# Decoder trunk on one core: pooled loads issued by the ACT queue three products apart, the last pooling mixer and the embedding inputs some products later

## The chip, the cores and the metric

The kernel runs on one core of a Trainium2 chip. The metric is the device time of one execution in microseconds (us). TensorE is called PE, VectorE DVE, ScalarE ACT, GpSimd POOL and SyncE SP. SP computes nothing here: it issues DMA transfers. ACT and POOL also issue some transfers, in the order in which their own instructions stand. PE multiplies weights that it loads 128x128 at a time with moving tiles of 128x512 elements.

## The reference, cut to what matters

A sequence of 1024 tokens of width 2048 goes through one layer. Names are those of the kernel, where `u` is the pooling mixer's input, `gp` and `ga` are the gates of the pooling and of the attention branch, and `cc` is the concatenated input of the output projection.

```python
h = x @ w_in + b_in
q, k, v, g_attn, u_pool, g_pool = split(h)
a = banded_sink_attention(q, k, v, sinks, bias, valid) * silu(g_attn)
b = multiscale_pool(u_pool, w_pool, pool_scale) * silu(g_pool)
mix = concatenate([a, b]) @ w_out
ple = sigmoid(x @ w_gate_ple) * (p @ w_ple)
out = layer_norm(ALPHA * x + mix + ple, ln_gain, ln_bias)
```

`multiscale_pool` subtracts each channel from its trailing mean over 2, 4, 8 or 16 tokens (four groups of 256 channels), maps each group with a 256x256 matrix of its own and scales the channels. All of it is in float32.

## The kernel before, in words

**Products.** A float32 product is made of three: each operand is split into a high part, which ACT casts (`wh`, `b11h`, `t1h`, ...), and a low part, which DVE gets by a subtraction (`wl`, `b11l`, ...). `mm3` (L179 to L181) issues high by high, low by high and high by low. Above this lies one level of Strassen's scheme in Winograd's form: two blocks of 128 output columns (a *job*) take seven products instead of eight. The right-hand operand is kept as seven sets with the names `b11`, `b21`, `t1`, `t2`, `t3`, `b22`, `t4`, and the left-hand (weight) operand is made for each job by DVE additions on the loaded `raw` tiles, followed by the split into `wh` and `wl` (`make_unit`). One product is a run of 12 matmuls of 128x512 into one PSUM bank (`qa` or `qb`). It is gathered into an SBUF tile `part`: the first one by an ACT copy (L346), the others by DVE additions (L122).

**Order.** A group is one job alone or two jobs side by side. `run_group` issues the products of a group one after the other, and after each of them a clock ticks. All other work is tied to that clock: `after(n, f)` calls `f` n products later, and `later(n, f)` does the same and also keeps what `f` issues behind the latest gathering instructions. A scheduler then puts the instructions of each engine in a row, so that a number of products says where a piece of work may stand, and the engine's queue, in order, says what stands behind it.

**The stage around the change.** Half 0 of the sequence goes through the last input projections (`gp`, `u`), then through eight `wgate` groups (the sigmoid gate of the embedding), then through `ga0` and `ga1` alone and `ga2`, `ga3` side by side. After that half 1 of `w_out` is multiplied by a right-hand set built from `cc4` to `cc7`, the *pooled set*.

* `pool_u` (L612) makes the trailing means of one group of channels. On its second call of a group it sets four things by the clock: a load of the map `wpool` and its split, a load of the gates (`s<-sgp`), and `mix(g)` (L641). `mix` is 24 matmuls (`sc<-e`), four DVE products (L653), and four stores that POOL issues (`cc<-s`). The last of the mixers is that of g = 1. The gates come from `gate_pool` (L604): ACT takes the silu of the finished `gp` tile, and SP stores it (`sgp<-part`).
* `embed_in` (L659) loads the four tiles of `p` (`s<-in_p`), two products apart, and splits them (L669 and DVE). `rest` multiplies them by `w_ple` (`sc<-e`) one to four products after a `wgate` group has ended; `embed_ahead` loads `x` for it (`s<-in_x`).
* The pooled set is built by `set_from` (L255): `begin` sets four fetches of two 512 KB tiles each (`two<-cc`, L267) by the clock, and the steps `s0` to `s4` split them (`b11h`, ...) and subtract them (`two<-two,two`). `pooled()` is called ahead of the last group but two, so that the loads fall into the groups `ga1` and `ga2`/`ga3`.
* `gate_ahead` loads the attention's results (`s<-pre`), and `gate_attn` (L597) takes silu and multiplies (DVE `part<-s,part`), after the DMA-accumulated first half has come in (`part<-h`, L359, issued by POOL).

**Slots.** The `s` tiles are 16 slots used in turn, and in the stage of the pooled set six smaller ones; `e` tiles are six. A load into a slot waits for the last reader of what lay there, and where that was a transfer, for its end. `raw` tiles and `wh`/`wl` tiles are used in turn as well.

Of the kernel before, what the change touches and what calls it, by code (L numbers as in the profile page):

```python
# [32 lines left out]
T = 512  # L33
# [30 lines left out]
class Layer:  # L64
# [78 lines left out]
    def fetch(self, src, extra=False):  # L143
        s = self.extra() if extra else self.slot()
        return self.load(s[:, : src.shape[-1]], src)

    def split(self, src, extra=False):
        n = src.shape[-1]
        hi, lo = ((self.extra if extra else self.slot)(F32R)[:, :n] for _ in range(2))
        self.nc.scalar.copy(out=hi, in_=src)  # L150
        self.lo(lo, src, hi)
        return hi, lo
# [10 lines left out]
    def later(self, n, fn):  # L163

        def run():
            with ExitStack() as ctx:
                for ins in self.latest.values():
                    ctx.enter_context(self.tc.issue_after(ins))
                fn()
        self.after(n, run)  # L170
# [81 lines left out]
    def two(self):  # L252
        return self.tile(self.twos, [P, 2, self.F], "two")

    def set_from(self, get, F, keep=None, first=None, by=None):  # L255

        nc = self.nc
        r = {}

        def fetch(u, part=None):  # L260
            h, k = int(u[2]) - 1, 2 * (int(u[1]) - 1)
            if not part:
                r[u] = [self.two() for _ in range(2)]
            for i, t in enumerate(r[u]):
                src = get(h, k + i)
                if part is None:
                    (by or (nc.sync if first else nc.scalar)).dma_start(out=t, in_=src)  # L267
                elif i == 0 and part < 2:
                    self.load(t[:, part], src[:, part])
                elif i == 1 and part == 2:  # L270
                    self.load(t, src)

        def sub(u, a, b, place):
            out = []
            for k in range(2):
                o = r[place][k] if place else self.two()
                self.tt(o, r[a][k], r[b][k], ALU.subtract)
                if keep:
                    self.load(keep[u][k], o)
                out.append(o)  # L280
            r[u] = out

        split = lambda u: self.split_unit(u, r[u])

        def begin():
            self.F = F
            if first:
                first(fetch)
                return
            for i, u in enumerate(("b11", "b21", "b12", "b22")):  # L290
                self.later(1 + 2 * i, lambda u=u: fetch(u))

        def s0():
            if first:
                a, b = r["b11"]
                self.split_unit("b11", [a[:, 0], a[:, 1], b])
            else:
                split("b11")

        def s1():  # L300
            split("b21")
            sub("t1", "b12", "b11", "b11")

        def s2():
            split("t1")
            sub("t2", "b22", "t1", None if keep else "t1")

        def s3():
            split("t2")
            sub("t3", "b22", "b12", "b12")  # L310

        def s4():
            split("t3")
            sub("t4", "b21", "t2", "b21")

        return [begin, s0, s1, s2, s3, s4, lambda: split("b22"), lambda: split("t4")]

    def set_kept(self, get, keep):
# [289 lines left out]
    def pool_u(self, j, c):  # L608
        nc, g = self.nc, j // 2
        w = 2 << g  # L610
        out = []
        for h in range(2):  # L612
            u = self.slot()
            if h == 0:
                nc.gpsimd.memset(u[:, 0:16], 0.0)
            else:
                self.ident_act(u[:, 0:16], c[:, 0, T - 16 :], self.c(C_BIN + U0 + j))
            self.ident_act(u[:, 16:], c[:, h], self.c(C_BIN + U0 + j))
            cur, d, first = u, 1, 1
            while d < w:  # L620
                nxt = self.slot()
                end = 2 * d == w
                f = 16 if end else first
                self.tt(nxt[:, f:], cur[:, f:], cur[:, f - d : T + 16 - d], ALU.add)
                cur, d = nxt, 2 * d
                first = first + d
            if h == 0:
                self.tt(cur[:, 16 : 16 + 16], cur[:, 16 : 16 + 16], self.c(C_HEAD + 16 * g, 16), ALU.mult, nc.gpsimd)
            nc.vector.scalar_tensor_tensor(out=cur[:, 16:], in0=cur[:, 16:], scalar=1.0 / w, in1=u[:, 16:],
                                           op0=ALU.mult, op1=ALU.subtract)  # L630
            out.append(self.split(cur[:, 16:], 2 * (j % 2) + h < 3))
        self.diff[j] = out
        if j % 2:
            f = slice((g % 2) * T, (g % 2) * T + T)
            self.after(4, lambda: self.got.update({("wp", g): self.fetch(self.wpool[g // 2][:, f])}))
            self.later(8, lambda: self.got.update({("wp", g): self.split(self.got["wp", g])}))
            late = 3 if g == 1 else 0
            self.after(6 + late, lambda: self.got.update({("sg", g): [[self.fetch(self.sgp[2 * g + e][:, h * T : h * T + T]) for e in range(2)] for h in range(2)]}))
            self.later(10 + late // 2, lambda: self.mix(g))

    def mix(self, g):  # L641
        nc = self.nc
# [182 lines left out]
    def run(self):  # L825
        nc, tc, fix = self.nc, self.tc, self.fix
# [28 lines left out]
        ga, gp, u = ([(win, *p) for p in pairs(b, 4)] for b in (GA0, GP0, U0))  # L855
# [60 lines left out]
        for o in reversed(BESIDE):  # L916
            u = UNITS[o]
# [61 lines left out]
        g = 2  # L979
# [13 lines left out]
        t = 9  # L993
# [12 lines left out]
        g += n2  # L1006


        pooled, *make_pooled = self.set_from(lambda h, k: self.cc[4 + k][:, :, h * T : h * T + T], T, by=nc.sync)
        for i in range(n3):  # L1010
            if i == 1:
                over.close()
                over = ExitStack()
                self.extras = self.work_pool("e2", 6, over)
            if self.groups[g + i + 1][0][0].b[0] == 0 and i < n3 - 2:
                self.after(5, self.embed_in)
                self.after(7, lambda: self.embed_w(0))
            if i == n3 - 2:

                over.close()  # L1020
                work.close()
                work = ExitStack()
                self.slot_n = T
                self.slots = self.work_pool("slots1", 6, work)
                self.twos = self.work_pool("twos1", 8, work)
                pooled()
                for n, step in enumerate(make_pooled):
                    self.after(10 + 3 * n, step)
                for n, b in enumerate(b for j in s3[-2:] for b in j.b):
                    self.after(14 + 2 * n, lambda b=b: self.gate_ahead(b - GA0))  # L1030
            self.run_group(g + i, () if i else steps)
# [86 lines left out]
        for k in range(4):  # L1118
            r = rest_x[k]
            f = slice((k % 2) * 2 * F2, (k % 2) * 2 * F2 + 2 * F2)  # L1120
            h, l = (t[k // 2][:, f].rearrange("p (k t) -> p k t", k=2) for t in (hi, lo))
# [92 lines left out]
```

## Time and profile before

| | |
|---|---|
| time before, median of 3 | 1492.81 us (1492.71 to 1498.43) |
| profiled execution, its own time | 1498.43 us |
| its span, first to last instruction | 1496.7 us |
| PE busy | 1450.5 us, 97% of the span |
| DVE, ACT, POOL busy | 75%, 52%, 19% |
| mean granted TensorE clock | 0.990 of full speed |

The profiled execution is the slowest of the three, 5.62 us above the median. Busy is the time in which an engine had an instruction. A matmul of 128x512 is listed with 0.39 us, while the next starts some 0.227 us later, since they are pipelined: start times are what is to be compared. In brackets behind a row stands how long the engine was idle before it, and what released it. A row with x2 stands for two such instructions one after the other.

### The profile page before, as it was taken

The numbers are of one execution on the slowest core, as the hardware profiler recorded it, in microseconds if no ns is written. First come the engines' busy times: TensorE is split into PE (matmuls) and PEld (weight loads), VectorE is DVE, ScalarE is ACT, GpSimd is POOL, SyncE is SP. The second block draws the span as 40 slices with busy tenths as digits, with TensorE's granted clock in tenths as the row PEclk, the third lists the DMA queues.
The fourth block names the chain that finished last, engine by engine and source line by source line (L and its number), as shares of the span: only waits on it lengthen the run. The fifth ranks groups of instructions, "written<-read, shape, count | busy, mean of one in ns | idle before, by whom it ended". The sixth has DMA issues, their size and how long they took to land. (4 is left out here: it accounts for less than half of the span.)

```text
span 1496.7 us, 20472 instructions
## 1 busy us (share of the span) xinstructions
PE 1450.5 (97%) x6972; PEld 1224.6 (82%) x6972; DVE 1120.8 (75%) x2030; ACT 780.7 (52%) x1550; POOL 277.7 (19%) x388
## 2 busy tenths in 40 slices
PE   8999999999999999999999999999999999999986
PEld 6788888888887888888887778888877888899985
DVE  7788578888787877888677956565579566987785
ACT  5354656655666555666634443333356333555484
POOL 0000123322333332231111110000011111111240
PEclk9999999999999999999999999999999999999998
DMA  7563975445445554557856666575696667585463
GB/s 262 190 218 102 258 197 191 148 150 184 171 171 176 170 188 174 174 191 250 197 140 202 158 219 190 170 193 166 197 295 183 172 187 224 146 231 137 155 230 137
DMA packets 101721, 280.38 MB, mean 187 GB/s; under 512 B 11632, under 2 KB 16880, under 8 KB 101616
## 3 DMA queue, kind: packets, MB, share of 16 engines
q1 hardware_dynamic: 78576, 204.09, 40.1%
q0 software_dynamic: 19712, 67.64, 19.5%
q10 hardware_dynamic: 3328, 7.34, 1.5%
q8 instruction: 55, 0.90, 0.2%
q14 instruction: 50, 0.41, 0.1%
HBM read 193.04 MB, written 85.98 MB: 186 GB/s over the span
## 5 line engine op out<-in xcount | busy, mean ns | idle before, releaser
L222 ACT CAST wh<-raw 128x512 fp32r<-128x512 f32 x428 | 263.7, 619 | 452.8 <-PE qa L180 145.1
L122 DVE TENSOR_TENSOR wl<-raw,wh 128x512 fp32r<-128x512 f32 x428 | 300.3, 706 | 135.9 <-ACT wh L222 130.5
L346 ACT COPY part<-qa 128x512 f32<-128x512 f32 (+1 forms) x180 | 103.7, 576 | 56.0 <-PE qa L181 51.8
L551 POOL TENSOR_SCALAR_AFFINE_SELECT s<-s 128x512 fp32r<-128x512 f32 x128 | 101.1, 802 | 144.5 <-ACT s L544 97.7
L122 DVE TENSOR_TENSOR part<-part,qb 128x512 f32<-128x512 f32 (+1 forms) x120 | 80.9, 674 | 48.5 <-PE qb L181 45.9
L179 PE MATMUL qa<-b11h,wh 128*128 128x512 f32 (+2 forms) x292 | 111.1, 381 | 2.7 <-ACT b11h L248 2.4
L181 PE MATMUL qa<-b11h,wl 128*128 128x512 f32 (+2 forms) x292 | 109.8, 377 | 0.7 <-DVE wl L122 0.6
L180 PE MATMUL qa<-b11l,wh 128*128 128x512 f32 (+2 forms) x292 | 109.9, 376 | 0.0
L181 PE MATMUL qb<-b21h,wl 128*128 128x512 f32 (+2 forms) x292 | 108.7, 372 | 1.1 <-DVE wl L122 1.1
L179 PE MATMUL qb<-b21h,wh 128*128 128x512 f32 (+2 forms) x292 | 109.1, 374 | 0.0
L180 PE MATMUL qb<-b21l,wh 128*128 128x512 f32 (+2 forms) x292 | 108.6, 372 | 0.0
L181 PE MATMUL qa<-t2h,wl 128*128 128x512 f32 (+1 forms) x260 | 101.0, 390 | 7.6 <-DVE wl L122 7.6
L179 PE MATMUL qa<-t2h,wh 128*128 128x512 f32 (+1 forms) x260 | 101.6, 391 | 4.4 <-ACT wh L222 2.5
L179 PE MATMUL qb<-t1h,wh 128*128 128x512 f32 (+1 forms) x260 | 102.0, 392 | 2.8 <-DVE part L122 1.9
L181 PE MATMUL qb<-t1h,wl 128*128 128x512 f32 (+1 forms) x260 | 100.7, 387 | 1.5 <-DVE wl L122 1.5
L179 PE MATMUL qa<-t3h,wh 128*128 128x512 f32 (+1 forms) x260 | 100.6, 387 | 0.0
L179 PE MATMUL qa<-t4h,wh 128*128 128x512 f32 (+1 forms) x260 | 100.4, 386 | 0.3 <-DVE part L122 0.3
L180 PE MATMUL qb<-t1l,wh 128*128 128x512 f32 (+1 forms) x260 | 100.6, 387 | 0.0
L180 PE MATMUL qa<-t2l,wh 128*128 128x512 f32 (+1 forms) x260 | 100.4, 387 | 0.0
L179 PE MATMUL qb<-b22h,wh 128*128 128x512 f32 (+1 forms) x260 | 100.4, 386 | 0.0
L180 PE MATMUL qa<-t3l,wh 128*128 128x512 f32 (+1 forms) x260 | 99.8, 384 | 0.0
L180 PE MATMUL qb<-b22l,wh 128*128 128x512 f32 (+1 forms) x260 | 99.7, 384 | 0.0
(286 smaller groups left out, 3557.6 us busy)
## 6 DMA issues: line engine op xcount, KB each, us to landing
raw<-in_win SPq DMA_DIRECT2D x65, 512.0 KB, 4.3
h<-part SPq DMA_DIRECT2D x34, 512.0 KB, 2.9
part<-h POOLq DMA_DIRECT2D x34, 512.0 KB, 6.3
cw<-in_wout SPq DMA_DIRECT2D x64, 256.0 KB, 3.0
raw<-in_wgate SPq DMA_DIRECT2D x32, 512.0 KB, 4.0
raw<-wc SPq DMA_DIRECT2D x32, 512.0 KB, 4.5
s<-in_x SPq DMA_DIRECT2D x44, 256.0 KB, 5.6
wc<-cw SPq DMA_DIRECT2D x32, 256.0 KB, 2.3
```

The costliest lines, as they stand in the source:

```text
L122: return (eng or self.nc.vector).tensor_tensor(out=out, in0=a, in1=b, op=op)
L179: mm(ps, wh, xh, start=start, stop=False, skip_group_check=True)
L180: mm(ps, wh, xl, start=False, stop=False, skip_group_check=True)
L181: return mm(ps, wl, xh, start=False, stop=stop, skip_group_check=True)
L222: self.unit_latest = [nc.scalar.copy(out=hi, in_=src).ins, L.lo(lo, src, hi).ins]
L346: self.mark("ACT", self.nc.scalar.copy(out=dst, in_=ps))
L551: nc.gpsimd.affine_select(out=o4, in_=a4, pattern=[[0, 4], [sign, P]], compare_op=ALU.is_ge, fill=0.0, base=0 if side else -1, channel_mul ...
```

## The change

The pooled set's loads were issued by SP (`by=nc.sync`), 1, 3, 5 and 7 products after `begin`; they are now issued by ACT, 1, 4, 7 and 10 products after it. For the last mixer (g = 1) the gates are fetched 10 products later instead of 9, and the mix is issued 13 products later instead of 11. `embed_in` is called after 8 products of its group instead of 5. Below line 637 the changed file is one line shorter.

```diff
-    def set_from(self, get, F, keep=None, first=None, by=None):
+    def set_from(self, get, F, keep=None, first=None, by=2):
...
-                    (by or (nc.sync if first else nc.scalar)).dma_start(out=t, in_=src)
+                    (nc.sync if first else nc.scalar).dma_start(out=t, in_=src)
...
-                self.later(1 + 2 * i, lambda u=u: fetch(u))
+                self.later(1 + by * i, lambda u=u: fetch(u))
...
-            late = 3 if g == 1 else 0
-            self.after(6 + late, lambda: self.got.update({("sg", g): ...
-            self.later(10 + late // 2, lambda: self.mix(g))
+            self.after(10 if g == 1 else 6, lambda: self.got.update({("sg", g): ...
+            self.later(13 if g == 1 else 10, lambda: self.mix(g))
...
-        pooled, *make_pooled = self.set_from(lambda h, k: self.cc[4 + k][:, :, h * T : h * T + T], T, by=nc.sync)
+        pooled, *make_pooled = self.set_from(lambda h, k: self.cc[4 + k][:, :, h * T : h * T + T], T, by=3)
...
-                self.after(5, self.embed_in)
+                self.after(8, self.embed_in)
```

On SP, at the last mixer and the first `wgate` group (place A), the row before is: the last gate, the fourth tile of `p`, four tiles of `x`, a tile of `w_ple` and two weight tiles.

```order
L136 DMA s_8719<-sgp_165 128x512
L136 DMA s_8721<-in_p 128x512
L136 DMA s_8763<-in_x 128x512
L136 DMA s_8765<-in_x 128x512
L136 DMA s_8768<-in_x 128x512
L136 DMA s_8770<-in_x 128x512
L136 DMA s_8912<-in_wple 128x512
L136 DMA raw_8879<-in_wgate 128x1024
L136 DMA raw_8901<-in_wgate 128x1024
```

The same place now, where `s_8736` is the third tile of `p` and `s_8790` the fourth:

```order
L136 DMA s_8734<-sgp_165 128x512
L136 DMA s_8736<-in_p 128x512
L136 DMA s_8761<-in_x 128x512
L136 DMA s_8763<-in_x 128x512
L136 DMA s_8766<-in_x 128x512
L136 DMA raw_8863<-in_wgate 128x1024
L136 DMA s_8768<-in_x 128x512
L136 DMA s_8790<-in_p 128x512
L136 DMA raw_8901<-in_wgate 128x1024
L136 DMA s_8912<-in_wple 128x512
```

The fourth tile of `p` has moved from ahead of the four tiles of `x` to behind them and a weight tile. The slot of the fourth tile of `x`, `s_8768`, is that of the mixer's first gate, from which POOL stores to `cc5`.

On ACT, at the same place, the row before holds the four casts of `p` (L669) together, ahead of the copy that frees the bank `qa`:

```order
L346 COPY part_8604<-qa_8609 128x512
L669 CAST e_8808<-s_8573 128x512
L669 CAST e_8812<-s_8623 128x512
L669 CAST e_8816<-s_8666 128x512
L669 CAST s_8820<-s_8721 128x512
L222 CAST wh_8844<-raw_8427 128x512
L346 COPY part_8824<-qa_8830 128x512
L222 CAST wh_8862<-raw_8302 128x512
```

Now, where `s_8877` is the cast of the fourth tile of `p` and `e_8869` that of the second:

```order
L346 COPY part_8602<-qa_8607 128x512
L222 CAST wh_8792<-raw_8427 128x512
L346 COPY part_8770<-qa_8776 128x512
L222 CAST wh_8846<-raw_8302 128x512
L222 CAST wh_8883<-raw_8427 128x512
L346 COPY part_8770<-qa_8776 128x512
L668 CAST e_8865<-s_8643 128x512
L668 CAST s_8877<-s_8790 128x512
L668 CAST e_8869<-s_8692 128x512
L682 ACT_TABLE_LOAD
L682 ACTIVATE part_8601<-part_8601 128x1024
```

The casts of `p` stand behind the casts and copies of the first three products of the second `wgate` group, and that of the fourth tile is ahead of that of the second.

On ACT, where the pooled set is loaded (place B, the end of `ga1` and the begin of `ga2`/`ga3`), the row before has no load; `part_10339` is the last tile of `ga1`, `part_10500` and `part_10502` those of `ga2` and `ga3`:

```order
L222 CAST wh_10452<-raw_10224 128x512
L222 CAST wh_10469<-raw_10035 128x512
L222 CAST wh_10504<-raw_10224 128x512
L346 COPY part_10339<-qa_10344 128x512
L222 CAST wh_10527<-s_2073_10522 128x512
L346 COPY part_10500<-qa_10508 128x512
L222 CAST wh_10550<-s_2077_10545 128x512
L346 COPY part_10502<-qa_10531 128x512
L248 CAST b11h_10568<-two_10358 128x1024
L248 CAST b11h_10568<-two_10359 128x1024
```

Now:

```order
L222 CAST wh_10448<-raw_10224 128x512
L267 DMA two_10358<-cc_224 128x2x512
L267 DMA two_10359<-cc_225 128x2x512
L267 DMA two_10427<-cc_226 128x2x512
L267 DMA two_10428<-cc_227 128x2x512
L222 CAST wh_10465<-raw_10035 128x512
L346 COPY part_10339<-qa_10344 128x512
L267 DMA two_10492<-cc_224 128x2x512
L267 DMA two_10493<-cc_225 128x2x512
L222 CAST wh_10500<-raw_10224 128x512
L346 COPY part_10496<-qa_10504 128x512
L346 COPY part_10498<-qa_10527 128x512
```

Four loads stand ahead of the copy of `part_10339`, two more ahead of the next cast; the last two follow. On SP the eight loads are gone, so that the first four `s<-pre` follow directly on the weight tiles. By the semaphores of the program the fourth, fifth, seventh and eighth of ACT's loads each wait for the landing of one of these four `s<-pre`.

On DVE, at place B, the row before the four products `part<-s,part` of `ga1` is:

```order
L122 TENSOR_TENSOR wl_10551<-s_2077_10545,wh_10550 128x512
L122 TENSOR_TENSOR raw_10224<-raw_10224 128x512
L122 TENSOR_TENSOR b11l_10569<-two_10358,b11h_10568 128x1024
L122 TENSOR_TENSOR part_10500<-part_10500,qb_10554 128x512
L122 TENSOR_TENSOR b11l_10569<-two_10359,b11h_10568 128x1024
L122 TENSOR_TENSOR part_10338<-s_10487,part_10338 128x512
L122 TENSOR_TENSOR part_10338<-s_10489,part_10338 128x512
L122 TENSOR_TENSOR part_10339<-s_10492,part_10339 128x512
L122 TENSOR_TENSOR part_10339<-s_10494,part_10339 128x512
L122 TENSOR_TENSOR wl_10583<-raw_10035,wh_10582 128x512
```

Now, where `part_10498` is the gathering of the second product of `ga3`:

```order
L122 TENSOR_TENSOR part_10498<-part_10498,qb_10586 128x512
L122 TENSOR_TENSOR raw_10397<-raw_10224,raw_10397 128x512
L122 TENSOR_TENSOR wl_10547<-s_2075_10541,wh_10546 128x512
L122 TENSOR_TENSOR raw_10224<-s_2075_10541,raw_10224 128x512
L122 TENSOR_TENSOR b11l_10569<-two_10358,b11h_10568 128x1024
L122 TENSOR_TENSOR raw_10224<-raw_10224 128x512
L122 TENSOR_TENSOR b11l_10569<-two_10359,b11h_10568 128x1024
L122 TENSOR_TENSOR part_10338<-s_10483,part_10338 128x512
L122 TENSOR_TENSOR part_10338<-s_10485,part_10338 128x512
L122 TENSOR_TENSOR part_10339<-s_10488,part_10339 128x512
L122 TENSOR_TENSOR part_10339<-s_10490,part_10339 128x512
L122 TENSOR_TENSOR wl_10583<-raw_10035,wh_10582 128x512
```

The gathering of `ga3`'s second product stood behind `wl_10583` and now stands seven DVE rows ahead of the four `part<-s,part`. On PE, the `t1` products of `ga2` and `ga3` now stand one after the other ahead of the first `t2` product; before, `ga2`'s first `t2` product began between them. The mixer's 24 matmuls stand 24 matmuls later: behind the `b11` and `b21` products of the second `wgate` group instead of ahead of them. POOL's row is in the same order as before.

## Rows read from the trace of the kernel before

**Rows 1.** The page: busy time, share of the span and instructions of each engine.

```profile
PE 1450.5 (97%) x6972; PEld 1224.6 (82%) x6972; DVE 1120.8 (75%) x2030; ACT 780.7 (52%) x1550; POOL 277.7 (19%) x388
```

**Rows 2.** Waits of PE from 1080 to 1170 us: us in total, times, longest us.

```profile
PE qa L181 <- DVE wl L122: 3.8, 2, 3.4
PE qb L179 <- DVE part L122: 1.1, 1, 1.1
PE qa L179 <- ACT wh L222: 1.0, 1, 1.0
```

**Rows 3.** Timeline of PE at place A: start us, us, engine, line, operation, out<-in, in brackets the idle time before it and its releaser.

```profile
871.42 0.39 PE L179 MATMUL sc<-e,s 128*128 128x512 f32 x1
...
875.36 0.39 PE L181 MATMUL sc<-s,s 128*128 128x512 f32 x1
877.63 0.50 PE L179 MATMUL sc<-e,s 128*128 128x512 f32 x1 [1.88 <-DVE s L653]
...
885.90 0.50 PE L179 MATMUL qa<-t2h,wh 128*128 128x512 f32 x1 [1.11 <-ACT part L346]
...
891.48 0.39 PE L179 MATMUL sc<-e,s 128*128 128x512 f32 x1
```

**Rows 4.** Timeline of ACT, DVE, SP and POOL at place A, same columns; SPq rows and POOL's DMA rows are issues.

```profile
876.83 0.75 DVE L653 SCALAR_TENSOR_TENSOR s<-sc,cst,s 128x512 f32<-128x512 f32 x1 [2.00 <-DMA s<-sgp]
...
884.22 0.62 ACT L669 CAST s<-s 128x512 fp32r<-128x512 f32 x1 [5.21 <-DMA cc<-s]
...
885.27 0.58 ACT L346 COPY part<-qa 128x512 f32<-128x512 f32 x1
...
873.86 4.67 SPq L136 DMA_DIRECT2D s<-in_x  x4
...
874.18 0.58 POOL L141 DMA_DIRECT2D cc<-s  x1 [0.34 <-issue]
```

**Rows 5.** DMA issues: operation xcount, KB each, median us from issue to landing; the first row is the one store issued at 874.18 us, the second the one load of `p` issued at 873.27 us, the last two are those of the whole span.

```profile
cc<-s POOLq DMA_DIRECT2D x1, 256.0 KB, 10.0
...
s<-in_p SPq DMA_DIRECT2D x1, 256.0 KB, 7.9
...
cc<-s POOLq DMA_DIRECT2D x16, 256.0 KB, 4.7
...
s<-in_p SPq DMA_DIRECT2D x4, 256.0 KB, 4.6
```

**Rows 6.** Timeline of PE at place B.

```profile
1100.16 0.39 PE L179 MATMUL qa<-b11h,wh 128*128 128x512 f32 x1
...
1108.32 0.39 PE L179 MATMUL qb<-t1h,wh 128*128 128x512 f32 x1
...
1111.04 0.44 PE L179 MATMUL qa<-t2h,wh 128*128 128x512 f32 x1
...
1115.13 0.80 PE L181 MATMUL qa<-t2h,wl 128*128 128x512 f32 x1 [3.41 <-DVE wl L122]
...
1118.39 0.39 PE L179 MATMUL qb<-t1h,wh 128*128 128x512 f32 x1
```

**Rows 7.** Windows: the stretch, its length, busy us (instructions) of PE, PEld, DVE, ACT and POOL, the granted clock, the DMA share and GB/s.

```profile
870.00:880.00 10.00, 8.12 (x36) 6.31 (x35) 6.43 (x11) 3.23 (x6) 3.47 (x5) 1.00 0.88 212
...
1115.00:1118.00 3.00, 2.87 (x6) 2.13 (x7) 3.00 (x6) 0.00 (x0) 0.56 (x1) 0.50 1.06 391
...
1150.00:1160.00 10.00, 7.49 (x29) 4.94 (x28) 8.98 (x15) 5.43 (x8) 1.28 (x3) 0.96 0.49 195
1160.00:1170.00 10.00, 10.00 (x40) 8.16 (x39) 6.01 (x8) 3.32 (x6) 0.00 (x0) 0.87 0.18 47
```

**Rows 8.** Timeline of DVE, ACT and SP at place B.

```profile
1105.32 1.22 DVE L122 TENSOR_TENSOR b11l<-two,b11h 128x1024 fp32r<-128x1024 f32 x1
...
1111.82 2.65 DVE L122 TENSOR_TENSOR part<-s,part 128x512 f32<-128x512 f32 x4 [3.55 <-DMA s<-pre]
1114.39 0.68 DVE L122 TENSOR_TENSOR wl<-raw,wh 128x512 fp32r<-128x512 f32 x1
...
1091.51 1.14 ACT L222 CAST wh<-raw 128x512 fp32r<-128x512 f32 x2
1097.94 0.58 ACT L346 COPY part<-qa 128x512 f32<-128x512 f32 x1
...
1088.33 8.00 SPq L267 DMA_DIRECT2D two<-cc  x6
1096.38 2.96 SPq L136 DMA_DIRECT2D s<-pre  x4
```

**Rows 9.** DMA issues of place B: the first row is the four issued from 1096.38 us, the next two are the two issues under way at 1096.0 us, the sixth `two<-cc` of SP and the first `part<-h` of POOL. The last row is from the view of line 267, min/median/max of one issue in ns.

```profile
s<-pre SPq DMA_DIRECT2D x4, 256.0 KB, 14.9
...
two<-cc SPq DMA_DIRECT2D x1, 512.0 KB, 15.5
part<-h POOLq DMA_DIRECT2D x1, 512.0 KB, 9.0
...
L267 ACTq DMA_DIRECT2D two<-cc x8: 525/606/1258, 1244.2 to 1261.1; - x8
```

**Rows 10.** Timeline of PE at another stage, 470 us: a longer idle time, and the windows row that holds it (columns as in rows 7).

```profile
470.67 0.66 PE L457 MATMUL tr<-ident,s 128*128 128x128 f32 x4 [2.77 <-DVE s L122]
...
466.00:478.00 12.00, 9.23 (x49) 7.43 (x48) 9.56 (x28) 8.44 (x24) 3.55 (x5) 1.00 0.41 153
```

More of the change, by code (lines that the diff above doesn't have):

```diff
@@ L636, in pool_u @@
             self.later(8, lambda: self.got.update({("wp", g): self.split(self.got["wp", g])}))
-            late = 3 if g == 1 else 0
-            self.after(6 + late, lambda: self.got.update({("sg", g): [[self.fetch(self.sgp[2 * g + e][:, h * T : h * T + T]) for e in range(2)] for h in range(2)]}))
-            self.later(10 + late // 2, lambda: self.mix(g))
+            self.after(10 if g == 1 else 6, lambda: self.got.update({("sg", g): [[self.fetch(self.sgp[2 * g + e][:, h * T : h * T + T]) for e in range(2)] for h in range(2)]}))
+            self.later(13 if g == 1 else 10, lambda: self.mix(g))
     def mix(self, g):
```

## The prediction
> **What bounds the kernel now.** I read the page's busy shares first: PE is busy for 97% of the span [rows 1], so the end is set by PE's own row of matmuls, and only what holds PE up counts. Next come PE's waits and the timeline around them. Starts of matmuls lie 2.72 us apart per product (1108.32 to 1111.04 for twelve, 0.227 each) [rows 6]. The change touches two places.
>
> At place A (the last mixer) PE waits twice: 1.88 us inside the mixer and 1.11 us behind it [rows 3]. A row is listed with 0.39 us while the pace is 0.227, so a wait costs its idle time, 0.16 us of lost overlap and about 0.1 for the slow first matmul (0.50): 2.15 and 1.4, together 3.5 us.
>
> At place B (pooled set) PE waits 3.41 us at 1115.13 [rows 2, 6]. Its third `t2` matmul was due at 1111.04 + 2 x 0.227 = 1111.5, so 3.6 us are lost. The clock is then 0.50 from 1115 to 1118, the 1.2 GHz level [rows 7]: seven matmuls from 1115.13 take until 1118.39, 3.26 us instead of 1.59, 1.7 more. B1 costs 5.3 us. A second group of short waits follows after 1150: 2.5 us of 10 without PE work, and granted clocks of 0.96 and 0.87 in ten us each, 0.4 + 1.3 us more [rows 7]: B2, about 4.2 us.
>
> All four sum to 13 us, 0.9% of the span. A measurement of this kernel can tell about 0.5%, 7.5 us, from no change.
>
> **Place A, what goes.** The first wait ends with DVE's product at 876.83, which waited for the gates' loads (`s<-sgp`) [rows 4]. The mixer moves 24 matmuls later, from 871.42 to 871.42 + 24 x 0.227 = 876.9, and needs its second gate at about 879.5; the loads were there at 876.8. The second wait ends with the ACT copy at 885.27, which stood behind the cast of `p`'s fourth tile, 5.21 us late, because that tile's slot was to be freed by a mixer store (`cc<-s`) [rows 4]. In the new order the copy stands ahead of the casts. Both waits go: 3.5 us gained. The fetch of the gates one product later hides behind the same move.
>
> **Place A, what comes.** The fourth tile of `p` is now loaded behind the fourth of `x`, whose slot the mixer's first store to `cc5` must leave. That store: the mixer's first bank is done at 876.9 + 6 x 0.23 = 878.3, DVE takes 0.75, POOL issues at about 879.4. It landed after 10.0 us before, when it was queued beside four loads of `x`; the 16 such stores of the whole program take 4.7 [rows 5]. I take 4.8, since the `x` tiles go out no later than before and so some 5 us ahead of that store: 884.2. Then two SP issues (4.67 us for four includes waits, 0.4 to 0.5 for one is what `p` took) put `p` out at 884.9. It lands after 4.6 (median of its four) or 7.9 (the one at this place) [rows 5]: I take 4.6, 889.5. On ACT the cast of the second tile stands behind that of the fourth, so that PE's embedding products stop after three matmuls until two casts (0.53 apart) and a DVE subtraction (0.68) are done, at 891.3. They are due at 876.9 + 5.5 + 24 x 0.227 = 887.9, three matmuls later 888.6: 2.7 us, and 0.3 for the restart. The bounds: at the good end the tile lands before 886.8 and nothing stalls; at the bad end the store takes 10.0 and the load 7.9, which puts the landing at 890.1 + 7.9 = 898 and the stall at 11 us. The store of 10.0 was issued among the `x` loads and this one is not, so I stay near the medians. Net at A: 3.5 - 3.0 = 0.5 us gained, between 3.5 gained and 8 lost.
>
> **Place B, what goes.** DVE sat idle for 3.55 us before the four products `part<-s,part`, until the loads `s<-pre` landed [rows 8]: issued at 1096.38 behind six loads of the pooled set that SP took 8.00 us to issue, and landed after 14.9 [rows 8, 9]. Now they follow the weight tile and go out as soon as their slots are free; by the casts ahead of them in the program I put that at 1092.7. They will have landed long before 1108, so this idle time goes.
>
> **Place B, what comes.** First, DVE's row has changed: the gathering of `ga3`'s second product (done on PE at 1108.3) stands seven rows ahead of the four products, and the split that PE's third `t2` matmul waits for stands behind them. From 1108.4: gathering 0.6, two additions of weights 1.3, a split 0.6, `b11l` twice 2.3, one more addition 0.6, four products 2.6, the split 0.68 (row times 1.22, 2.65 and 0.68 less some 0.08 of overlap each) [rows 8]: 1117.0. On PE both `t1` products now come ahead of `t2`, so the matmul is due at 1108.32 + 24 x 0.227 + 0.45 = 1114.2. It waits about 2.8 us, and 0.2 for the restart. Does the clock fall? The idle times of 1.88 us (granted clock 1.00 in 870 to 880) and 2.77 us (1.00 in 466 to 478) left it, that of 3.41 did not [rows 3, 6, 7, 10]. At 2.7 it probably stays. B1 then costs 3.0 instead of 5.3: 2.3 us gained.
>
> Second, eight issues on ACT. An ACT issue of such a load takes 525 to 1258 ns, 606 at the median [rows 9]: 4.8 us for eight, bounds 4.2 to 10. ACT is idle for half of this stretch; behind the first four, issued from 1092.6 (the casts of 1091.51 end there [rows 8]), stand a cast and the copy that frees PE's bank for `ga3`'s first product at 1100.16 [rows 6]. Without a wait that copy comes at 1097.94 as before [rows 8]: no cost.
>
> Third, a new wait: the fourth load waits for the first `s<-pre` to land. That must happen by about 1098.5 (1100.16 less an issue, a cast and a copy), within 5.8 us of its issue. Before, 14.9 us passed, but in SP's own queue behind six loads: the sixth of them, issued at 1096, landed after 15.5 us, and a `part<-h` of twice the size of an `s<-pre`, which POOL issued at the same time, after 9.0 [rows 9]. Transfers of another engine's queue pass a full one; half of 9.0 is 4.5, so I take the wait as just met and its cost at nothing, with 9 us at the other end (a landing at 1107.5, copy at 1109).
>
> The Trainium skill ("DMA: Bandwidth & Descriptors") bears on this with two rules that point apart. Its section "Queues, rings and completion order" says each DMA engine takes turns between the queues that have work, a packet at a time; by that `s<-pre` gets its share at once, and the sum stands as above. Its section "Issuing engines are not separate DMA queues" says that transfers run on the same 16 engines whoever issues them, and only issue time is saved; by that the load of 4 MB is merely moved, and `s<-pre` may land as late as before, the slower case below. The two rows of 1096 agree with the first.
>
> B2 stays: its chain of products, store and copy hangs on the same DVE row, which is full there (8.98 of 10 us) [rows 7], and all of it comes earlier with B1. Net at B: 2.3 gained.
>
> **The sum.** 0.5 + 2.3 = 2.8 us gained: 1498.43 - 2.8 = 1495.6 for the profiled execution. It lies 5.62 us above the median, so it may hold waits that the other two runs lack. Taken off the median, 1492.81 - 2.8 = 1490.0.
>
> **The rivals.**
>
> *Both places come clean.* The fourth `p` lands in 3 us, the casts do not meet PE, and DVE, free of its wait, works ahead. For it: the gates and `s<-pre` get more than five us of air. Against it: DVE's row at B takes 8.6 us between two fixed points of PE that are 5.9 apart. Gain 3.5 + 5.3, with B2 also 13: 1484 to 1480.
>
> *The fourth `p` is late.* The store takes 10.0 us or the load 7.9. For it: both did so at this very place before [rows 5]. Against it: fewer transfers beside them. A late load alone ends the stall at 894.6 (6.3 us), a late store alone at 896.5 (8.2): A loses 2.8 to 4.7 net, and a fall of the clock 1.7 more; B gains 2.3: 1495 to 1497.
>
> *ACT is blocked, slower than before.* The fourth load on ACT waits until `s<-pre` lands, and the copy behind it holds PE's product of 1100.16. It decides from a landing later than 1098.5 on. With 14.9 us from 1092.7 the copy comes at 1109, PE waits 9 us and the clock falls (1.7), while B1 goes (5.3): 5 us lost with A's 0.5 taken off: 1497.7. Against it: `s<-pre` stands first in its queue.
>
> *It does nothing here.* The runs at the median lack these waits, and the edits move only what is hidden: 1492.8.
>
> **How the numbers follow.** Forecast 0.45; both clean 0.16; `p` late 0.19; ACT blocked 0.13; nothing 0.07. Faster by over 0.5% (under 1485.3) is most of the clean case: 0.14. Slower (over 1500.3) needs ACT blocked and `p` late together, or a new wait after them: 0.07. Within 0.5%: 0.79. The range leaves out half of the clean case's and a little of the blocked case's end: 1482.5 to 1498; the forecast's own is 1487 to 1493.
>
> **What would show it.** At A: no wait of PE inside the mixer; one at the embedding's fourth matmul, released by an ACT or DVE split, behind an `s<-in_p` issued after 884. At B: `s<-pre` issued near 1093 and landed within 6 us; DVE without idle time ahead of `part<-s,part`; PE's wait at `t2` of 2 to 3 us, clock 1.00 behind it; the short waits after 1150 still there. It is wrong if ACT's row shows a gap ended by `s<-pre` with PE waiting on a copy (L346), if the wait at the embedding exceeds 5 us, or if a place outside A and B changes by over 2 us.

## The result and the profile after

| | before | changed |
|---|---|---|
| median of 22 runs each | 1493.24 us | 1499.03 us |
| ratio, 95% interval | | 1.0033 [1.0025, 1.0041] |
| profiled execution: span | 1496.7 us | 1497.6 us |

The change is 5 us slower (0.0033 x 1493); 2.8 us faster was forecast. The two profiled spans differ by 0.9 us only. That of before belongs to the slowest of its 22 runs, and comparing the starts of the same matmuls shows why it hides the loss: by 860 us, ahead of all that was changed, the changed kernel's execution is already 3.5 us earlier. Between places A and B of the prediction, and behind them, both keep the same distance to within 0.3 us. So each place is compared by itself, by how long PE takes from one product ahead of it to one behind it. That gives 3.0 us lost at A and 1.8 at B, together the 5 us.

**Place A after.** PE's timeline, the counterpart of [rows 3]:

```profile
884.88 0.40 PE L181 MATMUL sc<-e,s 128*128 128x512 f32 x1
889.04 0.80 PE L179 MATMUL sc<-e,s 128*128 128x512 f32 x1 [3.76 <-ACT e L668]
...
893.85 0.55 PE L180 MATMUL qa<-t3l,wh 128*128 128x512 f32 x1
894.23 0.39 PE L181 MATMUL qa<-t3h,wl 128*128 128x512 f32 x1
```

Both waits of before are gone, and a new one stands at the embedding's fourth matmul. Behind it the clock is at the 1.2 GHz level (the window 889 to 893, columns as in [rows 7]):

```profile
889.00:893.00 4.00, 3.95 (x9) 2.80 (x10) 2.40 (x5) 3.99 (x5) 0.00 (x0) 0.50 0.02 8
```

The chain that led there, in the timelines of POOL, SP and ACT ([rows 4] before):

```profile
876.16 0.58 POOL L141 DMA_DIRECT2D cc<-s  x1 [5.78 <-DVE s L652]
...
869.75 1.78 SPq L136 DMA_DIRECT2D s<-in_x  x3
874.97 0.33 SPq L136 DMA_DIRECT2D raw<-in_wgate  x1
882.14 0.33 SPq L136 DMA_DIRECT2D s<-in_x  x1
882.56 0.38 SPq L136 DMA_DIRECT2D s<-in_p  x1
...
887.85 0.62 ACT L668 CAST s<-s 128x512 fp32r<-128x512 f32 x1 [4.55 <-DMA s<-in_p]
```

SP stands from 875.3 to 882.14, until the mixer's first store has landed (5.9 us after its issue). The tile of `p` goes out behind it and lands 5.3 us later.

**Place B after.** First PE's waits, then rows of ACT, DVE and POOL, which answer to [rows 6, 8]:

```profile
1100.20 0.50 PE L179 MATMUL qa<-b11h,wh 128*128 128x512 f32 x1 [0.36 <-ACT part L346]
1117.15 0.50 PE L181 MATMUL qa<-t2h,wl 128*128 128x512 f32 x1 [2.12 <-DVE wl L122]
1123.67 0.50 PE L179 MATMUL qa<-t3h,wh 128*128 128x512 f32 x1 [1.68 <-ACT part L346]
...
1156.89 0.50 PE L179 MATMUL qa<-t2h,wh 128*128 128x512 f32 x1 [1.66 <-ACT wh L222]
1159.77 0.50 PE L181 MATMUL qa<-t2h,wl 128*128 128x512 f32 x1 [2.14 <-DVE wl L122]
```

```profile
1099.05 0.62 ACT L222 CAST wh<-raw 128x512 fp32r<-128x512 f32 x1 [6.87 <-DMA s<-pre]
...
1102.46 0.62 ACT L222 CAST wh<-raw 128x512 fp32r<-128x512 f32 x1 [2.31 <-DMA two<-cc]
...
1107.96 1.05 ACT L248 CAST b11h<-two 128x1024 fp32r<-128x1024 f32 x1 [2.84 <-DMA s<-pre]
...
1122.03 0.58 ACT L346 COPY part<-qb 128x512 f32<-128x512 f32 x1 [5.01 <-PE qa L181]
...
1108.72 0.69 DVE L122 TENSOR_TENSOR part<-part,qb 128x512 f32<-128x512 f32 x1 [0.17 <-PE qb L181]
...
1111.13 1.22 DVE L122 TENSOR_TENSOR b11l<-two,b11h 128x1024 fp32r<-128x1024 f32 x1
...
1114.01 2.49 DVE L122 TENSOR_TENSOR part<-s,part 128x512 f32<-128x512 f32 x4
...
1115.90 0.56 POOL L141 DMA_DIRECT2D cc<-part  x1 [14.44 <-DVE part L122]
```

ACT stands twice until an `s<-pre` lands, and once (2.31 us) until its own second load has landed, for which its sixth load waits. The long wait of [rows 6] has shrunk to 2.12 us and the clock does not fall behind it (granted 1.00 from 1117 to 1120), as forecast. But `b11l` starts at 1111.13 instead of 1105.32 and `part<-s,part` at 1114.01 instead of 1111.82. A wait on a copy has come at 1123.67, and the group after 1150 has grown: waits of 1.66 and 2.14 us where before [rows 2] had 1.0 and 0.4 (the 1.1 of [rows 2] has become two waits of 0.4).

The wait at 1123.67 hangs on `part<-s,part`: behind these four products POOL stores `ga1`'s result (`cc<-part`, issued at 1115.90, landed after 6.0 us). The copy of `qb` on ACT waits for that landing, since it writes into the slot that the store reads, and goes at 1122.03 (the profile names PE's product, which ended at the same time; in e2 and e7 it names the store). The copy of `qa` that frees PE's bank stands behind it. Before, the store went out at 1113.73.

### The profile page after: what moved, and what is told of

Its sections match the earlier page's. It is cut to its first block, busy times and chain, and to the rows that moved or that the text cites. A ratio compares the mean times of both kernels' runs of the same rounds, so it can differ in the third digit from the quotient of the medians.

```text
span 1497.6 us, 20472 instructions
## 1 busy us (share of the span) xinstructions
PE 1449.1 (97%) x6972; PEld 1223.0 (82%) x6972; DVE 1119.1 (75%) x2030; ACT 780.5 (52%) x1550; POOL 278.6 (19%) x388
## 5 line engine op out<-in xcount | busy, mean ns | idle before, releaser
L181 PE MATMUL qa<-t3h,wl 128*128 128x512 f32 (+1 forms) x260 | 100.1, 385 | 0.0
```

The source lines that it names most:

```text
L181: return mm(ps, wl, xh, start=False, stop=stop, skip_group_check=True)
```

## Experiments

Edits are to the kernel before, unless said otherwise. The table has what the profiles of all runs show: how much longer (+) or shorter PE took through each place than in the profile of before, from the starts of the same products. A is 850 to 905 us, B1 1090 to 1130, B2 1145 to 1175. Its first row shows by how much a place differs from one execution to another where nothing was changed, so that a single number is good to some 1.5 us.

| run | place A | B1 | B2 |
|---|---|---|---|
| place as before: A in e2, e5, e6, e7; B in e1, e3, e4, e9 | -1.1 to +0.8 | -1.6 to +1.4 | -1.8 to +0.2 |
| mixer later (e3, e8, e10) | -3.5 | | |
| mixer and `p` later (changed, e1, e11) | +3.0, +2.8, +2.8 | | |
| the same, `p` one product apart (e9) | -3.5 | | |
| `p` later alone (e4) | +0.6 | | |
| loads on ACT (changed, e2) | | -0.3, +2.3 | +2.1, +3.0 |
| loads on ACT, four `s<-pre` on POOL (e7) | | -0.4 | +1.8 |
| loads on POOL (e6) | | +2.8 | -1.0 |
| loads on SP, three apart (e5, e8, e11) | | -3.7, -3.8, -3.3 | -1.5, 0.0, -1.5 |
| loads on SP, from 4 products on (e10) | | -4.1 | -1.5 |

**Parts alone (e1 to e4).** First theory: the loss is made at place A, as the changed profile suggests. Rival: by ACT's loads.

e1:

```diff
-            self.after(6 + late, lambda: ...
-            self.later(10 + late // 2, lambda: self.mix(g))
+            self.after(10 if g == 1 else 6, lambda: ...
+            self.later(13 if g == 1 else 10, lambda: self.mix(g))
...
-                self.after(5, self.embed_in)
+                self.after(8, self.embed_in)
```

> Place A of the change alone: the mixer and the embedding's inputs later, the pooled loads as before. Theory A (the loss is made at place A: the fourth tile of p waits behind the fourth of x for a mixer store): about 3.2 us slower than before, ratio 1.002, and a PE wait of 3 to 4.5 us at the embedding's fourth matmul with the clock at the 1.2 GHz level behind it. Theory B (the loss is made by the pooled loads on ACT): 3 us faster or the same, 0.998 to 1.000.

Measured 1.0009 [0.9995, 1.0023]. The wait is there (3.28 us, granted clock 0.50 behind it), but the price of the whole part is between 0.7 us gained and 3.4 lost.

e2 (`gap` is the spacing):

```diff
-                self.later(1 + 2 * i, lambda u=u: fetch(u))
+                self.later(1 + gap * i, lambda u=u: fetch(u))
...
-        ..., T, by=nc.sync)
+        ..., T, by=nc.scalar, gap=3)
```

> Place B of the change alone: pooled loads on ACT, three products apart. Theory A: about 1.4 us slower than before, ratio 1.001; PE's wait at the third t2 matmul 2 us instead of 3.4, later waits longer. Theory B: about 5 us slower, 1.003.

Measured 1.0033 [1.0020, 1.0047]: the rival's number. The first theory had the sizes wrong: place B alone costs 3 to 7 us. ACT with two apart was not run. In that program's order six loads instead of four stand ahead of the copy of `part_10339`, so whether the spacing counts on ACT stays open.

e3 has the mixer's two lines of e1 alone:

```diff
+            self.after(10 if g == 1 else 6, lambda: ...
+            self.later(13 if g == 1 else 10, lambda: self.mix(g))
```

e4 has the embedding's line alone:

```diff
-                self.after(5, self.embed_in)
+                self.after(8, self.embed_in)
```

> Only the mixer and its gates' fetch later; the embedding's inputs as before, with the fourth tile of p loaded ahead of all tiles of x. Theory A: both waits of place A go and no new one comes, 3 to 3.5 us faster, ratio 0.998. Rival (it is the mixer's later stores that hold up the embedding whatever the order of its loads): a new PE wait of 3 us or more at the embedding, ratio 1.001 or more.

> Only the embedding's inputs later; the mixer where it was. Theory A: the mixer's own wait of 1.9 us stays, that of the copy goes (1.4 gained), and a new wait of 1 to 4 us comes at the embedding, since the fourth tile of p is again behind the fourth of x: 0 to 3 us slower, 1.000 to 1.002. Rival (the later loads are harmless by themselves): 1.4 us faster, 0.999.

e3: 0.9982 [0.9966, 0.9997], no wait of PE over 0.2 us between 840 and 1100. e4: 0.9995 [0.9982, 1.0009], with a wait of 1.81 us at the embedding; its time fits both expectations, the wait the first. The mixer's move gains, and with the embedding's inputs later as well (e1) the gain is gone. The rival of e3 falls.

**Which row makes place A's wait (e9).** To e1 this is added:

```diff
-                self.after(1 + 2 * i, lambda i=i: r.append(self.fetch(self.p[i // 2][:, i % 2])))
+                self.after(1 + i, lambda i=i: r.append(self.fetch(self.p[i // 2][:, i % 2])))
```

> Place A as in run e1_mix_embed, with one edit: the four tiles of p are fetched one product apart instead of two, so that SP issues the fourth ahead of the gates and of all x tiles. The rows of ACT, DVE, PE and POOL are those of e1. If the wait at the embedding's fourth matmul comes from the fourth tile standing behind the store-bound x tile, it vanishes and place A gains the 3.5 us of e3: 0.997 to 0.9985. If it comes from the casts standing late on ACT, the wait stays at 3 us and the ratio at e1's 1.001.

Measured 0.9989 [0.9976, 1.0003], a little above the range expected, and at place A 3.5 us less than before. Only SP's row differs from e1. Its profile, ACT's timeline and the window:

```profile
883.11 0.62 ACT L668 CAST e<-s 128x512 fp32r<-128x512 f32 x1
883.63 0.62 ACT L668 CAST s<-s 128x512 fp32r<-128x512 f32 x1
```

```profile
884.00:894.00 10.00, 10.00 (x45) 8.09 (x44) 8.24 (x14) 6.62 (x10) 0.00 (x0) 1.00 0.37 118
```

The cast follows at once; PE is full. Place A is settled: the load of `p` behind the store-bound load of `x` makes the wait.

**ACT, the spacing, or SP's row (e5 to e8).** Both have e2's `gap`; e5 and e6 differ in the engine:

```diff
-        ..., T, by=nc.sync)
+        ..., T, by=nc.sync, gap=3)     (e5)
+        ..., T, by=nc.gpsimd, gap=3)   (e6)
```

> Place B: the spacing of three products alone, SP still issues. The rows of ACT, DVE and PE are those of before; on SP the four s<-pre go out behind four loads instead of six. If the loss of place B comes from ACT as issuer (held up or re-ordered): no loss here, 1 to 4 us faster, 0.997 to 0.999, PE's wait at the third t2 matmul below 3 us. If it comes from the loads' later times: slower, 1.002 to 1.003.

Measured 0.9956 [0.9939, 0.9973], 6.6 us faster: more than expected. SP, DVE and PE in its profile:

```profile
1089.33 5.91 SPq L267 DMA_DIRECT2D two<-cc  x4
1095.29 4.10 SPq L136 DMA_DIRECT2D s<-pre  x4
...
1110.43 2.50 DVE L122 TENSOR_TENSOR part<-s,part 128x512 f32<-128x512 f32 x4 [1.16 <-DMA s<-pre]
...
1113.58 0.49 PE L181 MATMUL qa<-t2h,wl 128*128 128x512 f32 x1 [0.91 <-DVE wl L122]
```

The landing of these four `s<-pre`, as in [rows 9]:

```profile
s<-pre SPq DMA_DIRECT2D x4, 256.0 KB, 14.1
```

With `s<-pre` behind four loads instead of six, DVE's wait falls from 3.55 [rows 8] to 1.16 and PE's from 3.41 to 0.91; by the table B1 gains 3.7 us. They take about as long to land as before (14.1 us, 14.9 in [rows 9]), but go out earlier: SP spends 5.91 us on the loads ahead of them instead of 8.00 [rows 8].

> Place B: the loads issued by POOL, three products apart. The rows of ACT, DVE and PE are those of before, and SP's row has lost the loads as in the changed kernel. If ACT as issuer makes the loss: 0.997 to 1.000. If the loss comes from taking the loads out of SP's queue (other transfers pass them, part<-h late): 1.002 to 1.004.

Measured 1.0021 [1.0009, 1.0032]: slower, with ACT's, DVE's and PE's rows as before. POOL, ACT and PE:

```profile
1102.48 0.89 POOL L359 DMA_DIRECT2D part<-h  x1 [1.42 <-DVE raw L122]
1105.76 0.89 POOL L359 DMA_DIRECT2D part<-h  x1 [2.39 <-issue]
...
1110.09 1.15 ACT L597 ACTIVATE part<-part,cst 128x1024 f32<-128x1024 f32 x1 [5.46 <-DMA part<-h]
...
1114.35 0.80 PE L179 MATMUL qa<-t2h,wh 128*128 128x512 f32 x1 [4.42 <-ACT wh L222]
```

POOL's own `part<-h` go out at 1102.48 and 1105.76 behind the new loads (1096.02 and 1098.93 before), and ACT waits for them and PE for ACT's cast behind. So it is not ACT alone: whichever engine issues, what stands behind the loads in its row waits with them.

e7 keeps e2's loads on ACT and moves four other loads:

```diff
-        self.got["ga", j] = [self.fetch(self.pre[j][:, h * T : h * T + T]) for h in range(2)]
+        r = [self.slot() for h in range(2)]
+        for h, s in enumerate(r):
+            (self.aside if j in (2, 3) else self.load)(s[:, :T], self.pre[j][:, h * T : h * T + T])
+        self.got["ga", j] = [s[:, :T] for s in r]
```

> Place B with ACT as issuer as in the changed kernel (place A as before), but the four s<-pre that ACT's loads waited for are issued by POOL: the rows of ACT, DVE and PE are those of run e2_only_set, and ACT's loads wait for nothing that is under way. Theory held (the loss is ACT's queue standing still for s<-pre): most of the 5 us goes, 0.999 to 1.001. Theory order (the loss is the changed order of the rows on ACT, DVE and PE): 1.002 to 1.0035, with the same waits after 1145 us as in e2.

Measured 1.0015 [1.0001, 1.0030], between both theories. PE's waits and a row of ACT in e2, then the same with a row of POOL in e7:

```profile
1100.61 0.50 PE L179 MATMUL qb<-b21h,wh 128*128 128x512 f32 x1 [1.35 <-ACT wh L222]
1114.08 0.79 PE L181 MATMUL qa<-t2h,wl 128*128 128x512 f32 x1 [2.69 <-DVE wl L122]
1153.21 0.50 PE L179 MATMUL qa<-t2h,wh 128*128 128x512 f32 x1 [1.59 <-ACT wh L222]
1156.09 0.80 PE L181 MATMUL qa<-t2h,wl 128*128 128x512 f32 x1 [2.15 <-DVE wl L122]
...
1099.94 0.62 ACT L222 CAST wh<-raw 128x512 fp32r<-128x512 f32 x1 [8.22 <-DMA two<-cc]
```

```profile
1110.80 0.50 PE L179 MATMUL qa<-t2h,wh 128*128 128x512 f32 x1 [1.81 <-ACT wh L222]
...
1151.17 0.49 PE L179 MATMUL qa<-t2h,wh 128*128 128x512 f32 x1 [1.83 <-ACT wh L222]
1154.05 0.80 PE L181 MATMUL qa<-t2h,wl 128*128 128x512 f32 x1 [2.15 <-DVE wl L122]
...
1109.09 1.15 ACT L600 ACTIVATE part<-part,cst 128x1024 f32<-128x1024 f32 x1 [2.96 <-DMA part<-h]
...
1099.22 0.90 POOL L359 DMA_DIRECT2D part<-h  x1 [6.12 <-ACT part L346]
```

ACT's longest stand-still in e2, 8.22 us, is the one for its own second load, not one for an `s<-pre`; the edit of e7 takes away that wait too. Without them PE's waits of 1100 and of the third `t2` matmul go, and a smaller one of 1.81 comes, with the clock at 0.59 for 3 us. That one is e7's own: POOL, which now issues the four `s<-pre`, stands 6.12 us ahead of its second `part<-h`, ACT waits 2.96 us for that, and the cast that PE waits for stands behind. The waits after 1150 stay as in e2. Those are in all three profiles with ACT's rows of the change and in none with those of before (0.8 to 1.0 and at most 0.4 there): they go with the changed order of the rows on ACT, DVE and PE. Which of the moved rows makes them was not tried. Since the intervals of e2 and e7 overlap and e7 has a wait of its own, how the 5 us divide between stand-still and order stays open.

**Together (e8, e10, e11).** e8 has the edits of e3 and e5, e11 those of e1 and e5 (the whole change with the loads left on SP). e10 adds to e8 a later start of the pooled loads:

```diff
-                self.later(1 + gap * i, lambda u=u: fetch(u))
+                self.later((4 if by else 1) + gap * i, lambda u=u: fetch(u))
```

> The mixer later as in e3 and the spacing of three on SP as in e5. If both places are independent, their gains add: e3 gave 2.7 us, e5 by expectation 1 to 4: 0.995 to 0.9975. Rival (what PE gains at A is lost in waiting for transfers at B, which do not come earlier): no more than e3 alone, 0.998.

> As e8_sp_gap3_mix, with the pooled loads starting 4 products after begin instead of 1: on SP the four s<-pre stand behind two loads instead of four; all other rows are the same. If PE's wait at the third t2 matmul follows the number of loads ahead of s<-pre (six: 3.4 us, four: 0.7 to 0.9), it goes to nothing, and the time is 0 to 2 us below e8: 0.9935 to 0.9945. If the loads that now come later are missed by the splits, new waits on b11 or b21 take it back: 0.995 to 0.998.

> The whole change with one part undone: SP issues the pooled loads, still three products apart. If ACT as issuer is what makes the change slow, place A's cost (1 to 3 us, e1) and place B's gain (6.6 us, e5) add up: 3.5 to 5.5 us faster, 0.9963 to 0.998. If the parts don't add, about the same as before, 0.999 to 1.001.

e8: 0.9945 [0.9930, 0.9961], the gains add. e10: 0.9941 [0.9927, 0.9956], the best kernel, 8.8 us below before; PE's wait at the third `t2` matmul is 0.60 us (0.69 in e8), not nothing, and the difference to e8 is inside the interval. The wait no longer follows the number of loads: in e10 `s<-pre` lands after 8.2 us (14.4 in e8), and DVE's products wait for something else, ACT's step behind `part<-h`:

```profile
1105.54 1.29 DVE L122 TENSOR_TENSOR part<-s,part 128x512 f32<-128x512 f32 x2 [0.84 <-ACT part L597]
```

e11: 0.9979 [0.9968, 0.9991], 3.1 us faster, in the range expected: taking ACT out of the change turns it from a loss into a gain.

## Why the prediction was wrong

**Place A, what goes: right.** By 879 us PE had gained 3.5 us over before's profile (3.5 forecast); e3 has it all.

**Place A, what comes: the mechanism right, its size wrong.** The wait came at the matmul, behind the store, the load and the cast that the step names. The store took 5.9 instead of 4.8, the load 5.3 instead of 4.6, and PE stood 3.76 us instead of 2.7. The step had no term for the clock: after the wait 18 matmuls from 884.42 took 10.7 us to the next embedding product at 895.14 instead of 4.1. So the wait cost 6.6 us, not 3.0: 3.9 of standing and 2.7 at the low clock. A lost 3.0 by the profiles (1.3 by e1's median) instead of gaining 0.5. The rival with a late `p` had this size at A (2.8 to 4.7 lost, before the clock), though neither the load nor the store was as late as it supposed: the clock made up for it.

**Place B, the first item: right as far as it goes, but it stops too early.** DVE's idle time went, DVE's new order put the split at 1117.1 (1117.0 forecast), the wait at `t2` was 2.12 us (2.7 to 2.8 forecast) and the clock held. The same order put `part<-s,part` 2.2 us later, and the sum ended at the `t2` matmul. It had no term for what stands behind these products: the store `cc<-part`, the copies on ACT that wait for it, and PE's 1.68 us at 1123.67. That path is read from the changed profile; no run undid it alone.

**Place B, the third item: its wait came, and its cost was put at nothing.** It took the wait for `s<-pre` as "just met and its cost at nothing". It was met as estimated: the first `s<-pre` landed 6.2 us after its issue, at 1098.40 (1098.5 forecast), and PE stood 0.36 us at the copy of 1100.16, 0.7 us lost. The waits of the fifth, sixth and eighth load were not priced either. In this profile they cost PE nothing that shows: DVE's gathering at 1108.72 waits for PE, not for ACT, and from there its row runs without idle time, as the forecast has it. In e2 the sixth load's wait did cost: 1.35 us of PE at 1100.61.

**"B2 stays": this step failed.** It grew: PE took 1.8 to 3.0 us longer there in all three profiles with ACT's rows of the change, while with the rows as before it differed by -1.8 to +0.2. I read the new order at the four products only and took the rest of the group as the old one moved earlier. ACT, DVE and PE had been re-ordered up to 1160, and after 1145 DVE had no reserve (9.61 of 10 us busy from 1150 to 1160):

```profile
1150.00:1160.00 10.00, 5.41 (x21) 3.28 (x20) 9.61 (x17) 6.42 (x10) 1.83 (x4) 1.00 0.47 188
1160.00:1170.00 10.00, 10.00 (x38) 8.06 (x38) 8.10 (x11) 3.21 (x7) 0.00 (x0) 0.83 0.06 22
```

In sum: forecast 0.5 gained at A and 2.3 at B; the changed profile has 3.0 lost at A and 1.8 at B. The medians of the parts put it at about 1 (e1) and 5 (e2), so the division between the places is known only roughly. By the profile B is 4.1 us off the forecast: 0.7 at the copy, 1.9 at the wait of 1123.67 and 2.1 in B2, less 0.6 because the wait at `t2` was shorter. The slower rival had the right place and the wrong price: it set PE's loss at the copy at 9 us, where it was 0.7. That its sum of 1497.7 lies near the measured time is luck.

The prediction sets two rules of the Trainium skill ("DMA: Bandwidth & Descriptors") against each other: a DMA engine takes turns between the queues that have work (section "Queues, rings and completion order"), and issuing from another engine saves issue time alone (section "Issuing engines are not separate DMA queues"). The changed profile agrees with the first. These two loads were issued within 0.02 us of each other, ACT's first, which has twice the size:

```profile
two<-cc ACTq DMA_DIRECT2D x1, 512.0 KB, 9.7
s<-pre SPq DMA_DIRECT2D x1, 256.0 KB, 6.2
```

The median of the first four `s<-pre` was 9.1 us, against 14.9 in SP's own queue behind six loads [rows 9]. But behind two loads in SP's own queue it was 8.2 (e10), so the number of loads ahead counts as well, and no run separates the two.

## What to carry to other kernels

A wait that an engine's queue takes on can be paid by every instruction behind it: price the whole row up to the next slack, and through stores and copies as well, not the first instruction that PE needs. When a tuned order changes on several engines, look for a variant that changes one queue only: here the same loads three apart on SP moved four `s<-pre` ahead of two loads, changed no other row, and gained what the change was after. And a load behind one that waits for a store is as late as the store, however early its own data are there.

## What was not expected of the hardware

The clock fell behind waits of about 2.7 us in one place and not in another: granted 0.50 after 3.28 us (e1) and 3.76 (changed), 0.51 after 2.69 (e2), but 1.00 after 2.57 (e1, B1) and after the 2.77 of [rows 10]. It fell to 0.50 after 2.15 us (e2 and e7 after 1153), where another wait of 1.6 to 1.8 us lay 3 us ahead. It also fell after 2.30 us in e8, where PE had been busy without a wait for the 30 us ahead:

```profile
1143.12 0.77 PE L179 MATMUL qb<-t1h,wh 128*128 128x512 f32 x1 [2.30 <-ACT part L597]
...
1143.00:1146.00 3.00, 2.88 (x7) 2.33 (x8) 2.98 (x5) 2.05 (x3) 0.53 (x1) 0.50 0.00 0
```

In e4 (place A) and e7 (at 1110.80) it fell behind 1.81 us only: 0.65 from 888 to 891, and 0.59 from 1110.8 to 1113.8. A wait that costs 2 us by itself can cost 4 or 5 with the clock (in e2 the three us from 1156 had 0.50 and the next three 0.53), and the length of that one wait does not tell which.
